# Writing the halves of the split weights for the gates, z and C 64 bytes further on than the others

## Chip, cores and metric

The kernel runs on one core of a Trainium2 chip. The metric is device time in microseconds (us) of one execution. The core has a matrix engine (TensorE; its matmuls are PE in the profile, its weight loads PEld), VectorE (DVE), ScalarE (ACT), GpSimd (POOL) and SyncE (SP, which issues most DMAs). A matmul here multiplies a *stationary* block of 128 x 128 values, which a weight load brings into the array first, by a *moving* block of 128 x N values that is streamed through it. The result is added into a bank of the accumulation memory.

## What is computed

Two layers over 256 latent tokens of width 2048 (and 256 context tokens, which only the first layer reads). In each layer the input is normalised, modulated and multiplied by a large weight matrix; the parts of the product go through different branches, and a second matrix brings the result back to 2048 columns.

```python
p = h @ w_in                      # layer 0: q, gate, z, k, v, x, B, C, dt: 14400 columns
pc = hc @ w_in[:, base:]          # the context needs k, v, x, B, dt
ya = neighbourhood_attention(q, k, v, kc, vc, rpb) * silu(gate)
yb = gated_group_rmsnorm(y_ssd + d * x, z, ssm_norm_g)
x = x + gate0 * (concat([ya, yb]) @ w_out)
...
bg, cg, hv, g = split(h1 @ sc_w_in, 4)        # layer 1
x = x + gate1 * ((silu(g) * bg * dw_conv(cg * hv)) @ sc_w_out)
```

The gates of the attention, z and C are needed for the 256 latent tokens alone; x, B, k and v for latent and context tokens, 512 in all.

## The kernel before

**Split operands.** Each fp32 operand of a large product is split in two fp32r halves: H, a rounded copy, and L, the rest. A product is the sum of three matmuls: H by H, H by L and L by H. Weights come from memory in blocks of 1024 values a partition (`raw`). ScalarE copies `raw` into an H half (L417), VectorE subtracts it from `raw` into an L half (L424).

**Places.** There are three places for split weights (`NW = 3`, L162). Place k has two tiles of 128 x 1024, `wH{k}` (L167) and `wL{k}` (L168), so all six tiles stand one behind the other in the on-chip memory, each 4096 bytes a partition. `place()` takes the next free one, `split()` (L398) writes H, `low_part()` (L421) writes L, and `used()` (L474) gives the place back when all matmuls of the block are issued. In the first output projection three more places are added (L1826): one is the two halves of a single tile, `KL`; another the tiles `QT` and `QL`; the third two reused tiles.

**Two ways to multiply.** `mm_act` (L640) keeps the activations in the array and streams the weights, 512 columns at a time. `mm_ws` (L650) does the opposite: a block of 128 weight columns is stationary and the activations `hH[kb]` or `hL[kb]` move, with n = 512 columns (latent and context) for x and B, and with n = 256 (latent) for the gates (`do_g`, L1486), C and z (both in `do_ssd`, L1491). So the gates, z and C are all the projections that `mm_ws` does with n = 256, and no other projection has that form. A group of attention heads has four gate blocks and four z blocks of 128 columns and two C blocks, times 16 blocks of the contraction, times 4 groups, times three products.

The only other split matmuls with 256 moving columns are those of the attention's last step (L1117 to L1119): there `VH` and `VL` are stationary and `PH`, `PL` move, 12 matmuls a head.

**Where tiles lie.** Tiles are laid out one behind the other in the order in which the code declares them. Nearly all sizes are multiples of 128 bytes, and so `wH`, `wL`, `hH`, `hL`, `PH`, `PL`, `KL`, `QT` and `QL` all start at a multiple of 128 bytes. `VH` and `VL` are declared after some small tiles (`statq`, `gqk` and others) and start 96 bytes behind such a multiple.

**Order of the work.** The program is one fixed list an engine, written out by a planner in Python. Projections form the main line; every matmul calls `pump()`, which puts in steps of other tasks (heads, groups of the scan, norms, the matrix-vector product of the modulation) when the planner's clock says that their inputs are ready. A task begins only when as many `tmp` and `half` tiles are free as it declares (`begin`, L213; `budget`, L202). There are nine `half` tiles (`NHALF`, L162). A `group_gen` (L1371; two for each group of heads) holds four, then three, then two; a head takes one for its product; `make_c` two; `dt_gen` three.

The output projection of layer 0 goes through its 16 pairs of blocks in the order written at L540: pairs 0 to 5, 8 to 15, then 6 and 7. Pair 15 is the product of the last `group_gen`. For the first 1024 output columns a pair takes 24 matmuls.

Of the kernel before, what the change touches and what calls it, by code (L numbers as in the profile page):

```python
# [9 lines left out]
F32R = mybir.dt.float32r  # L10
# [7 lines left out]
COL_Q, COL_G, COL_Z, COL_K, COL_V, COL_X = 0, 2048, 4096, 6144, 8192, 10240  # L18
COL_B, COL_C, COL_DT = 12288, 13312, 14336
# [122 lines left out]
def kernel(ctx: ExitStack, tc, x, cx, ada0, w0, ada_w, ada_b, w_in, w_out, sc_in, sc_out, rpb, small, const,  # L142
# [12 lines left out]
    def st(shape, tag, dt=F32, name=None):  # L155
        return sb.tile(list(shape), dt, tag=tag, name=name or tag, bufs=1)
# [2 lines left out]
        return dr.tile(list(shape), F32, name="dram_" + name)  # L159


    NTMP, NHALF, NRAW, NW = 9, 9, 5, 3  # L162
    free_t = [st([128, 512], f"tmp{k}") for k in range(NTMP)]
    free_h = [st([128, 256], f"half{k}") for k in range(NHALF)]
    free_b = [pj.tile([128, 512], F32, tag=f"bank{k}", name=f"bank{k}", bufs=1) for k in range(8)]
    free_r = [st([128, 1024], f"raw{k}") for k in range(NRAW)]
    WH = [st([128, 1024], f"wH{k}", F32R) for k in range(NW)]  # L167
    WL = [st([128, 1024], f"wL{k}", F32R) for k in range(NW)]  # L168


    xrow = [st([128, D], "KT", name="x0")]
# [33 lines left out]
    def spawn(q, gen, tmps=0, halves=0):  # L205
        q.append(Task(gen, tmps, halves))
# [155 lines left out]
    def issue():  # L362

        while (loads or later) and (free_r or (loads and callable(loads[0]))):
            if loads and callable(loads[0]):
                loads.popleft()()
                continue
            if later and (not loads or (ngem[0] < loads[0][7] and len(RAW) - ngem[0] >= 5 - loads[0][7])):
                kind, key, w, r0, nb, c0, n = later.popleft()
                ngem[0] += 1  # L370
            elif loads:
                kind, key, w, r0, nb, c0, n, _ = loads.popleft()
            else:
                return
            raw = raw_()
            v = raw[:, :nb * n].rearrange("p (b c) -> p b c", b=nb)
            if w is ada0 or w is w0:
                E(DMA.dma_start(raw, w[r0]))
            else:
                E(DMA.dma_start(v, w[r0:r0 + nb * 128, c0:c0 + n].rearrange("(b p) c -> p b c", p=128)))  # L380
            RAW[key] = (raw, v)

    nw = [0]
    room = [2]

    def weight(w, r0, nb, c0, n):
        loads.append(("w", nw[0], w, r0, nb, c0, n, room[0]))
        nw[0] += 1
# [5 lines left out]
    def place():  # L394
        in_use.append(free_w.popleft())
        return in_use[-1]

    def split():  # L398
        k = pos["split"]
        raw, v = RAW.pop(k)  # L400
        nb, n = v.shape[1], v.shape[2]
        w = place()
        if n == 64:

            while lows:
                low_part()
            W = WH[w].rearrange("p (b c) -> p b c", b=nb)
            E(S.copy(W[:, :, :64], v))
            E(V.tensor_tensor(out=W[:, :, 64:], in0=v, in1=W[:, :, :64].bitcast(F32), op=ALU.subtract))
            HL[k] = (W, None)  # L410
            pos["split"] += 1
            give_raw(raw)
            issue()
            return
        H = WH[w][:, :nb * n].rearrange("p (b c) -> p b c", b=nb)
        Lo = WL[w][:, :nb * n].rearrange("p (b c) -> p b c", b=nb)
        E(S.copy(H, v))  # L417
        lows.append((k, H, Lo, v, raw))
        pos["split"] += 1

    def low_part():  # L421

        k, H, Lo, v, raw = lows.popleft()
        E(V.tensor_tensor(out=Lo, in0=v, in1=H.bitcast(F32), op=ALU.subtract))  # L424
        HL[k] = (H, Lo)
        give_raw(raw)
        issue()
# [5 lines left out]
    def split_half(b):  # L433

        raw, v = RAW[0]
        H, Lo = (w[0].rearrange("p (b c) -> p b c", b=2) for w in (WH, WL))
        E(S.copy(H[:, b], v[:, b]))
# [13 lines left out]
    def splits_try():  # L451
        if hold[0]:
            return
        lows_try()
        while free_w and pos["split"] in RAW:
            if plan.ready([RAW[pos["split"]][1]]) > max(plan.t["PE"], plan.t["ACT"]) + 300:
                return
            split()
            lows_try()

    def use(ahead=0):
        k = pos["use"] + ahead
        while pos["split"] <= k:
            while pos["split"] not in RAW:
                issue()
                if pos["split"] not in RAW:
                    force(lambda: pos["split"] in RAW, (urgent, side, back))
            split()
        while k not in HL:
            low_part()  # L470
        splits_try()
        return HL.pop(k)
# [16 lines left out]
    def q_proj(w, c0, nc_, rows=D):  # L489
        room[0] = 2 if w is w_in and c0 >= COL_K else 1  # L490
        nb = 1024 // nc_
        for r0 in range(0, rows, nb * 128):
            weight(w, r0, nb, c0, nc_)

    def give_raw(raw):
        if not (spare_names and started[0] and raw.tensor.name in spare_names):
            free_r.append(raw)
# [34 lines left out]
    for j in range(1, 8):  # L532
        w_seg(j, CK, CV)
        if j < 7:
# [6 lines left out]
    ssd_cols = lambda s: [(w_in, COL_B + s * 256, 256), (w_in, COL_C + s * 256, 256), (w_in, COL_X + s * 512, 512),  # L541
                          (w_in, COL_Z + s * 512, 512)]
    q_proj(w_in, CG(0), 512)
    for r0 in (0, 1024):
        weight(w_in, r0, 8, COL_DT, 64)
    for j_ in ssd_cols(0)[1:]:
        q_proj(*j_)
    for a in range(1, 4):
        qk = [(w_in, CQ(a), 512), (w_in, CK(a), 512)]
        gv = [(w_in, CG(a), 512), (w_in, CV(a), 512)]  # L550
        for j_ in qk + gv + ssd_cols(a) if a < 3 else qk + ssd_cols(a) + gv:
            q_proj(*j_)
# [144 lines left out]
    def ada_gen():  # L697
        bc = lambda ap: ap.unsqueeze(2).to_broadcast([128, 2, 2])
        for j in range(8):
# [36 lines left out]
            for ts in ((0, 1), (2,), (3,)) if j == 0 else ((0, 1, 2, 3),):  # L736
# [25 lines left out]
                if ts == (0, 1):  # L762
                    hold[0] = False
                    split()
                    split()
# [854 lines left out]
    def turn_gen():  # L1620
        yield when(lambda: n_back[0] >= 11.5 and attn[0] == 32 and ssd_done[0] == 8)
        for k in range(2):
            pt = st([128, 4, 256], f"PT{k}", name=f"late{k}")
            late[4 * k:4 * k + 4] = [pt[:, q, :] for q in range(4)]
            pts.append(pt)
        E(V.scalar_tensor_tensor(out=A1, in0=M1[:, 1], scalar=1.0, in1=P_("g1"), op0=ALU.add, op1=ALU.mult))
        for kp in range(0, KB, 2):
            yield when(lambda: ("x1", kp // 4) in got and (kp < 8 or len(passed) == 4))
            yield W_("PE", x1[0][:, kp * 128:(kp + 2) * 128], x1[1][:, kp * 128:(kp + 2) * 128], nb=1)
            pt = bank()  # L1630
            for b in range(2):
                for t in range(2):
                    turn(pt[:, b * 256 + t * 128:b * 256 + (t + 1) * 128], x1[t][:, (kp + b) * 128:(kp + b + 1) * 128])
            if kp == 14:
                yield when(lambda: ("h1", 7, 0) in got)
            for b in range(2):
                kb = kp + b
                if kp < 8 or kp == 14:
                    yield W_("ACT", pt)
                    E(S.activation(late[kb], pt[:, b * 256:(b + 1) * 256], AF.Copy, scale=A1[:, kb:kb + 1]))  # L1640
                else:

                    held[kb] = pt
                got.add(("turn", kb))
            if kp < 8 or kp == 14:
                give(free_b, pt)
# [131 lines left out]
    for ns in ((0, 512), (1024,), (1536,)):  # L1778
# [41 lines left out]
        if len(ns) == 2:  # L1820
            force(lambda: attn[0] == 32 and not side)
            x1 += [st([128, D], "KT", name="x1a"), st([128, D], "Vt", name="x1b")]
            for H, Lo in ((KL[:, 0:2], KL[:, 2:4]), (QT, QL), (st([128, 4, 256], "gt", F32R, name="wH5"), st([128, 4, 256], "sz", F32R, name="wL5"))):

                free_w.append(len(WH))
                WH.append(H.rearrange("p a b -> p (a b)"))  # L1826
                WL.append(Lo.rearrange("p a b -> p (a b)"))
            spawn(side, turn_gen())
# [98 lines left out]
    for i in range(4):  # L1927
        for part, gen in ((1, cg_gen), (2, hv_gen), (3, gg_gen), (0, bg_gen)):
            ps = banks(2)
            kb0 = 0  # L1930
            if i == 0 and part == 1:
# [3 lines left out]
                for t in range(2):  # L1935
                    for kb in range(8):
# [3 lines left out]
                        H, Lo = ws[kb // 2]  # L1940
# [110 lines left out]
```

## Time and profile before

| | |
|---|---|
| runs (us) | 1775.3, 1775.44, 1772.64; median 1775.3 |
| profiled execution, first to last instruction (its span) | 1770.0 us |
| the same execution's time around the span | not on the page; the median lies 5.3 us above the span |
| PE busy | 1749.4 us, 99% |
| DVE busy | 1262.5 us, 71% |
| ACT busy | 773.7 us, 44% |
| granted TensorE clock, mean | 0.999 |

Busy time of PE is no measure of its pace: matmuls overlap in the pipeline, and one that shows 0.28 us can be followed by the next after 0.12 us. The pace of matmuls, from start to start, is read from the starts in the timeline, or from a piece of the chain of waits that holds nothing but matmuls: its length divided by their count.

### The profile page before, as it was taken

The page shows a single profiled execution, that of the slowest core. Times are in us where ns is not written, and L with a number is a line of the kernel's source. Part 1 is how long each engine was busy: PE and PEld are TensorE (multiplying, and loading weights), DVE is VectorE, ACT ScalarE, POOL GpSimd, SP SyncE. Part 2 cuts the span into 40 slices and gives each one's busy share as a digit, 9 for nine tenths or more (in the row PEclk, how much of TensorE's full clock was granted, in tenths as well). Part 3 has the DMA queues.
Part 4 walks back from the last instruction along what each step waited for, and adds up shares of the span by engine and source line. Part 5 has one row for each costly group of instructions (what it writes and reads, how often), then busy time and mean ns, then how long its engine had stood idle before and what let it go on. Part 6 is the DMA issues. An engine that isn't in the chain of part 4 may idle for free.

```text
span 1770.0 us, 25382 instructions
## 1 busy us (share of the span) xinstructions
PE 1749.4 (99%) x9577; PEld 1472.7 (83%) x9577; DVE 1262.5 (71%) x1986; ACT 773.7 (44%) x1330; POOL 31.3 (2%) x28
## 2 busy tenths in 40 slices
PE   6999999999999999999999999999999999999998
PEld 4777988888888889888888898888888888888887
DVE  5656788878686878775878777786668777555554
ACT  5423544455242445342445343564546344444442
POOL 0000100001000001000001000000000000000000
PEclk9999999999999999999999999999999999999999
DMA  9977644666746666655666556658867787666563
GB/s 362 348 284 255 208 148 142 194 203 202 232 140 200 200 195 200 207 148 185 205 191 191 160 174 213 189 184 286 284 224 242 250 259 253 207 188 190 190 211 119
DMA packets 218138, 374.60 MB, mean 212 GB/s; under 512 B 32304, under 2 KB 69008, under 8 KB 218016
## 3 DMA queue, kind: packets, MB, share of 16 engines
q1 hardware_dynamic: 210704, 366.38, 64.1%
q10 hardware_dynamic: 7312, 6.61, 1.2%
q8 instruction: 75, 1.23, 0.3%
q14 instruction: 47, 0.39, 0.1%
HBM read 367.52 MB, written 6.72 MB: 211 GB/s over the span
## 4 chain that ended last, share of the span: by engine, by line
PE 97%; DMA 1%; DVE 1%; ACT 0%; SPq 0%; issue 0%; POOL 0%; DVEq 0%; ACTq 0%
PE bank L192 94%; PE bank L196 3%; DMA tmp<-dram_csr 1%; DMA raw<-in_ada 0%; DVE wL L424 0%; DVE acc L812 0%; SPq L578 0%; DVE tmp L1405 0%; DVE tmp L1416 0%; DVE tmp L598 0%; ACT wH L417 0%; DVE acc L798 0%; DVE half L1443 0%; ACT tmp L1401 0%; ACT half L719 0%
## 5 line engine op out<-in xcount | busy, mean ns | idle before, releaser
L417 ACT CAST wH<-raw 128x1024 fp32r<-128x1024 f32 (+1 forms) x375 | 392.0, 1046 | 586.1 <-PE bank L192 493.1
L424 DVE TENSOR_TENSOR wL<-raw,wH 128x1024 fp32r<-128x1024 f32 (+1 forms) x374 | 453.4, 1215 | 219.5 <-ACT wH L417 217.9
L192 PE MATMUL bank<-hH,wH 128*128 128x256 f32 (+1 forms) x1040 | 342.9, 330 | 0.0
L192 PE MATMUL bank<-hL,wH 128*128 128x256 f32 (+1 forms) x1040 | 336.8, 324 | 0.0
L192 PE MATMUL bank<-hH,wL 128*128 128x256 f32 (+1 forms) x1024 | 331.1, 323 | 0.0
L192 PE MATMUL bank<-wH,hH 128*128 128x512 f32 x640 | 256.4, 401 | 2.6 <-ACT hH L752 2.6
L192 PE MATMUL bank<-wL,hH 128*128 128x512 f32 x640 | 250.1, 391 | 0.0
L192 PE MATMUL bank<-wH,hL 128*128 128x512 f32 x640 | 249.8, 391 | 0.1
L812 DVE SCALAR_TENSOR_TENSOR acc<-raw,csil,acc 128x512 f32<-128x512 f32 x256 | 191.7, 749 | 62.3 <-DMA raw<-in_ada_w 55.6
L192 PE MATMUL bank<-wH,h 128*128 128x512 f32 x680 | 215.7, 391 | 0.0
L192 PEld LDWEIGHTS bank<-hH,wH 128*128 128x128 f32 x1040 | 197.7, 190 | 17.0 <-issue 2.2
L192 PEld LDWEIGHTS bank<-hL,wH 128*128 128x128 f32 x1040 | 197.9, 190 | 15.0
L192 PEld LDWEIGHTS bank<-hH,wL 128*128 128x128 f32 x1024 | 194.6, 190 | 15.7 <-DVE wL L424 0.4
L192 PEld LDWEIGHTS bank<-wH,h 128*128 128x128 f32 x680 | 127.6, 188 | 26.6 <-issue 0.2
L192 PEld LDWEIGHTS bank<-wH,hH 128*128 128x128 f32 x640 | 120.6, 189 | 30.6 <-issue 4.6
L192 PEld LDWEIGHTS bank<-wH,hL 128*128 128x128 f32 x640 | 120.4, 188 | 25.5 <-DVE hL L758 0.6
L192 PEld LDWEIGHTS bank<-wL,hH 128*128 128x128 f32 x640 | 120.7, 189 | 23.9 <-DVE wL L440 0.3
L192 PE MATMUL bank<-wH,mix 128*128 128x512 f32 x432 | 137.9, 392 | 0.0
L192 PE MATMUL bank<-wL,h 128*128 128x512 f32 x340 | 132.3, 389 | 0.0
L192 PEld LDWEIGHTS bank<-wH,mix 128*128 128x128 f32 x432 | 81.1, 188 | 16.7 <-issue 0.2
L192 PE MATMUL bank<-wL,mix 128*128 128x512 f32 x216 | 84.1, 389 | 0.0
L192 PEld LDWEIGHTS bank<-wL,h 128*128 128x128 f32 x340 | 63.9, 188 | 12.9
(284 smaller groups left out, 2168.2 us busy)
## 6 DMA issues: line engine op xcount, KB each, us to landing
raw<-in_w_in SPq DMA_DIRECT2D x196, 512.0 KB, 3.9
raw<-in_ada_w SPq DMA_DIRECT2D x128, 512.0 KB, 4.7
raw<-in_sc_in SPq DMA_DIRECT2D x128, 512.0 KB, 3.7
raw<-in_w_out SPq DMA_DIRECT2D x64, 512.0 KB, 4.9
raw<-in_ada SPq DMA_DIRECT2D x36, 512.0 KB, 5.9
raw<-in_sc_out SPq DMA_DIRECT2D x32, 512.0 KB, 4.1
PT<-in_ada SPq DMA_DIRECT2D x16, 512.0 KB, 8.9
tmp<-dram_csr SPq DMA_DIRECT2D x32, 256.0 KB, 6.4
```

The costliest lines, as they stand in the source:

```text
L192: E(T.matmul(o, l, r, start=start, stop=stop, skip_group_check=True))
L196: E(T.transpose(o, i, ident if k == 128 else ident[:k, :k]))
L417: E(S.copy(H, v))
L424: E(V.tensor_tensor(out=Lo, in0=v, in1=H.bitcast(F32), op=ALU.subtract))
L812: E(V.scalar_tensor_tensor(out=acc, in0=v[:, j], scalar=csil[:, 2 * k + j:2 * k + j + 1], in1=acc, op0=ALU.mult, op1=ALU.add))
```

## The change

The two tiles of a place become one tile of 2112 values, whose first 1024 are the old `wH` and next 1024 the old `wL`; 64 values are spare. For weight blocks of the gates, z and C, whose numbers `q_proj` notes in `shifted`, both halves start 16 values (64 bytes) later in the place. To pay for the spare room there is one `half` tile less. The three places grow by 768 bytes together and the `half` tiles shrink by 1024, so every tile declared after the places stands 256 bytes earlier.

```diff
-    NTMP, NHALF, NRAW, NW = 9, 9, 5, 3
+    NTMP, NHALF, NRAW, NW = 9, 8, 5, 3
...
-    WH = [st([128, 1024], f"wH{k}", F32R) for k in range(NW)]
-    WL = [st([128, 1024], f"wL{k}", F32R) for k in range(NW)]
+    places = [st([128, 2112], f"w{k}", F32R) for k in range(NW)]
+    WH = [t[:, :1024] for t in places]
+    WL = [t[:, 1024:2048] for t in places]
+    shifted = set()
...
-        H = WH[w][:, :nb * n].rearrange("p (b c) -> p b c", b=nb)
-        Lo = WL[w][:, :nb * n].rearrange("p (b c) -> p b c", b=nb)
+        H, Lo = (places[w][:, 16:1040], places[w][:, 1040:2064]) if k in shifted else (WH[w], WL[w])
+        H, Lo = (t[:, :nb * n].rearrange("p (b c) -> p b c", b=nb) for t in (H, Lo))
...
         for r0 in range(0, rows, nb * 128):
+            if w is w_in and (COL_G <= c0 < COL_K or COL_C <= c0 < COL_DT):
+
+                shifted.add(nw[0])
             weight(w, r0, nb, c0, nc_)
```

The blocks for dt (64 columns) and the block that `split_half` writes (L433) use `WH` and `WL` and stay where they were in the place.

## The prediction

> **What bounds the kernel now.** I read the page first, for the engines' shares and the chain of work that ended last.
>
> ```profile
> span 1770.0 us, 25382 instructions
> PE 1749.4 (99%) x9577; PEld 1472.7 (83%) x9577; DVE 1262.5 (71%) x1986; ACT 773.7 (44%) x1330; POOL 31.3 (2%) x28
> PEclk9999999999999999999999999999999999999999
> PE 97%; DMA 1%; DVE 1%; ACT 0%; SPq 0%; issue 0%; POOL 0%; DVEq 0%; ACTq 0%
> ```
>
> The chain is PE for 97% of the span, at the full clock. So the time is the number of matmuls times their pace from start to start, and there is hardly a wait to take out. What the change can move is the pace, and only where it moves an operand. The groups of matmuls by form give the count of those it aims at, and of those in the attention's last step, which have the same form:
>
> ```profile
> L192 PE MATMUL bank<-hH,wH 128*128 128x256 f32 x640 | 184.1, 288 | 0.0
> L192 PE MATMUL bank<-hH,wL 128*128 128x256 f32 x640 | 181.1, 283 | 0.0
> L192 PE MATMUL bank<-hL,wH 128*128 128x256 f32 x640 | 181.0, 283 | 0.0
> L192 PE MATMUL bank<-PL,VH 128*128 128x256 f32 x64 | 17.9, 280 | 0.0
> ```
>
> In these names the moving tile stands first, the stationary one second. The gates, z and C are 3 x 640 = 1920 matmuls with 256 moving columns; their stationary operands are the shifted halves. Their pace comes from the pieces of the chain of waits that hold nothing else, the first in the z projection, the second at the end of the kernel, where 512 columns move:
>
> ```profile
> 300.18 20.16 PE bank L192 x168
> 1683.20 82.32 PE bank L192 x363
> ```
>
> 20.16 / 168 = 120.0 ns for 256 columns, 82.32 / 363 = 226.8 ns for 512. Half of the second is 113.4: a short one takes 6.6 ns more than half a long one. Is that a fixed cost, or something that depends on where the operands lie? The trace holds one group that answers: in the attention's last step the moving tiles start at a multiple of 128 bytes, as everywhere, but the stationary `VH` and `VL` start 96 bytes behind one. Two of its runs of 12 matmuls in the timeline, each with the long matmul ahead of it and the one after it:
>
> ```profile
> 493.71 0.40 PE L192 MATMUL bank<-hH,wL 128*128 128x512 f32 x1
> 493.94 0.28 PE L192 MATMUL bank<-PH,VH 128*128 128x256 f32 x1
> ...
> 495.23 0.28 PE L192 MATMUL bank<-PH,VL 128*128 128x256 f32 x1
> 495.34 0.40 PE L192 MATMUL bank<-KT,QT 128*128 128x512 f32 x1
> ```
>
> ```profile
> 1179.42 0.40 PE L192 MATMUL bank<-wH,mix 128*128 128x512 f32 x1
> 1179.66 0.28 PE L192 MATMUL bank<-PH,VH 128*128 128x256 f32 x1
> ...
> 1180.94 0.28 PE L192 MATMUL bank<-PH,VL 128*128 128x256 f32 x1
> 1181.05 0.40 PE L192 MATMUL bank<-wH,mix 128*128 128x512 f32 x1
> ```
>
> From the first of the 12 to the matmul after them: 1.40 and 1.39 us, so 116.3 ns each by the rounded starts (0.01 us on either end is 0.8 ns); I use 116.5. That is 3.5 ns under the 120.0 of the same form with an aligned stationary operand. The weight loads tell the two apart as well, first the z projection from 302 to 319 us, then the attention's step:
>
> ```profile
> L192 PEld LDWEIGHTS bank<-hL,wH x48: 192/192/192, 301.8 to 318.7; 128*128 128x128 f32 x48
> L192 PEld LDWEIGHTS bank<-PL,VH x64: 187/187/189, 269.5 to 1180.7; 128*128 128x128 f32 x64
> ```
>
> All loads of the aligned weights take 192 ns there, each the same, while those of the offset ones take 187 to 189. A load runs beside the matmul before it. My reading: with both operands in the same phase the load's reads and the matmul's reads get in each other's way in the same manner every time, and the pair locks at 120.0; with another phase it doesn't lock.
>
> **The change part by part.**
>
> *The shift itself* is 64 bytes, not 96. No row of before shows 64, so the pace is bounded from both sides. Lowest: 113.4 ns, half of the long matmuls. Highest: a long matmul that has a load of `VH` beside it is followed after 0.23 and 0.24 us in the two runs above, together 0.47 against 2 x 226.8 = 454 ns, some 8 ns each too much; charged to every one of the 1920, the pace would be 128. Unchanged at 120.0 is possible as well. I take 116.5, by the nearest row, the only one in which a short matmul has an offset load beside it: 1920 x 3.5 = 6.7 us off. From this I take a tenth, an estimate, since the locked pace isn't everywhere: the hH,wH group averages 288 ns against 283 for its two neighbours, 5 x 640 = 3.2 us of breaks where other work is put in, and these stay. That leaves 6.0 us.
>
> *Who has to keep up.* In two of the z stretches VectorE is nearly full:
>
> ```profile
> 302.00:320.00 18.00, 18.00 (x152) 18.00 (x152) 17.79 (x23) 9.93 (x13) 0.00 (x0) 1.00 0.50 149
> 1028.00:1048.00 20.00, 20.00 (x169) 20.00 (x168) 19.72 (x26) 10.27 (x12) 0.00 (x0) 1.00 0.54 160
> ```
>
> (Columns: PE, PEld, DVE, ACT, POOL busy.) VectorE has 0.21 of 18 and 0.28 of 20 us left, 1.3%, while PE would become 2.9% faster. If the subtractions have no lead there, some 1.6% of these 38 us, 0.6 us, can't be had, since the next L half would be late. The lead is not nothing, so I take half of it: 0.3 us.
>
> *One tile for both halves.* The kernel has such a place already, `KL`, and its copy and subtraction cost what those of two tiles do:
>
> ```profile
> L417 ACT CAST wH<-raw 128x1024 fp32r<-128x1024 f32 x370 | 388.9, 1052 | 577.8 <-PE bank L192 489.4 <-issue 53.6 <-DMA raw<-in_w_in 6.9
> L417 ACT CAST KL<-raw 128x1024 fp32r<-128x1024 f32 x32 | 33.7, 1054 | 45.6 <-PE bank L192 41.3 <-DMA raw<-in_sc_in 2.3 <-issue 1.8
> L424 DVE TENSOR_TENSOR wL<-raw,wH 128x1024 fp32r<-128x1024 f32 x369 | 450.0, 1222 | 219.5 <-ACT wH L417 217.9
> L424 DVE TENSOR_TENSOR KL<-raw,KL 128x1024 fp32r<-128x1024 f32 x32 | 39.2, 1224 | 21.2 <-ACT KL L417 21.2
> ```
>
> A shifted H half reaches over the first 64 bytes of the old L half. Its copy must therefore wait for the last matmul that read that L, one matmul (0.12 to 0.23 us) later than before, when the place changes from unshifted to shifted. ScalarE waits on PE at L417 in any case (489.4 us in the row) and has 56% of the span free; behind the copy in its queue stand evacuations that are a microsecond early or late without harm, and the block is needed only after those of the two other places, 2 x 24 x 0.12 = 5.8 us later, against 1.05 + 1.22 us for copy and subtraction. Cost: nothing; without that cover, 0.2 us at 36 changes at most (twelve stretches, three places), 7 us.
>
> *One half tile less.* Two `group_gen` at a time hold 4 + 4; a head's product is the ninth. By the bookkeeping in the code the last `group_gen`, which takes all four remaining halves, would find three and begin when the head at work gives one back. The heads' products of that stretch lie 6.5 us apart (1140.56 and 1147.03), so it begins some 6 us late at most. Its result is pair 15, 14th in the order, due after 13 x 24 = 312 matmuls of the output projection:
>
> ```profile
> 1140.56 0.42 ACT L945 CAST mix<-half 128x256 fp32r<-128x256 f32 x1
> 1147.03 0.41 ACT L945 CAST mix<-half 128x256 fp32r<-128x256 f32 x1 [3.34 <-DVE half L1123]
> 1202.52 0.76 DVE L947 TENSOR_TENSOR mix<-half,mix 128x256 fp32r<-128x256 f32 x2
> 1127.00:1203.30 76.30, 64.22 (x267) 49.28 (x268) 5.35 (x14) 5.08 (x14) 1.00 0.63 201
> ```
>
> When it is written, at 1203.3, 267 matmuls on `mix` have run; 45 more at 0.227 are 10 us of lead. A delay of 6 is hidden. With no lead it would cost those 6 us.
>
> *Everything behind the places moves by 256 bytes.* Phases within 256 bytes stay as they are for all unshifted weights. Two of the three places then stand half of 512 bytes from the activations, which no row shows; I take nothing, with 8 ns a load as the upper end, as for the shift. The planner's order may change in places, worth 1 us either way by the size of the few PE waits left (the chain has 1% of DMA and 1% of DVE).
>
> **The sum.** 1770.0 - 6.0 + 0.3 = 1764.3 us of span. The median of the runs is 5.3 above the span of the profiled execution; with that, 1769.6.
>
> **The rivals.**
>
> *The full pace.* The lock goes and nothing takes its place: 113.4 ns, 1920 x 6.6 = 12.7 us, less a tenth and up to 0.9 us for VectorE: 10.5, so 1764.8. For it: the long matmuls show that the array can stream so. Against: the offset loads of before don't reach it, on average.
>
> *Nothing.* 64 bytes may be the same phase as 0: then 120.0 stays and the time is 1775.3, give or take the planner's 1 us. For it: 96 is 32 behind 64, so the rows of `VH` would also fit a phase of 64 bytes. Against: 16 values is a strange amount to see nothing from, but no row excludes it. The Trainium skill ("TensorE: Matmul & The Clock Gate", "Step-by-step: what each phase is for") gives the same result on another ground: the engine has two independent read ports, and "Loading the next tile's weights doesn't steal SBUF read bandwidth from the running matmul." By that rule 64 bytes would change no pace; the 120.0 against 116.5 and the loads of 192 against 187 speak against it here, though runs of 12 are short.
>
> *Slower: the load taxes the matmul.* The 8 ns that a long matmul pays with a load of `VH` beside it are paid by each matmul with a shifted load beside it: 1920 x 8 = 15.4 us, 1790.7. It decides as soon as the pace passes 120.0; from 122 on (3.8 us in all) it can be measured. For it: both hand-overs, and weights of all long projections are left unshifted. Against: inside the two runs each of 11 matmuls has such a load beside it and takes 116.5.
>
> *Slower: a stall at pair 15.* The late `group_gen` loses its lead as well: 6 us, with no gain 1781; against it stands the lead of 10 us.
>
> **How the numbers follow.** The forecast 0.42; full pace 0.18; nothing 0.15; taxed loads 0.18; a stall or another loss in the order 0.07. A measurement of this kernel tells about 0.2% (3.5 us) from no change. Faster by more: the first two, 0.60. Within: 0.15. Slower: 0.25. The range reaches from 1762, below the full pace, to 1781, where the stall ends; the taxed loads (0.18) are left out. The likeliest case alone: 1766 to 1772.
>
> **What would show it.** Right: pieces of z and gates in the chain of waits at about 116.5 ns a matmul instead of 120.0, their weight loads under 192 ns, the long pieces still at 226.8, L417 and L424 at 1052 and 1222 ns, PE at 99%. Wrong: 120.0 and 192 as before (nothing), a pace over 122 (taxed), long pieces away from 226.8 (the 256 bytes), a PE gap before 1214 us (pair 15), or VectorE at 100% with PE waits on `wL` in the z stretches.

## The result, and the profile after

| | before | after |
|---|---|---|
| median of 8 runs on one chip | 1774.86 us (1772.64 to 1777.18) | 1769.30 us (1765.40 to 1772.62) |
| ratio after / before | | 0.9971, 95% interval 0.9961 to 0.9981 |
| span of the profiled execution | 1770.0 us | 1766.2 us |

The change makes the kernel faster by 0.29% (0.19 to 0.39%). The forecast was 1769.6 us and 1764.3 us of span. The sum therefore came out nearly right, but two of its terms did not, and they erred in opposite directions: the pace gave more than was reckoned, and more waits stand in the profile of after. Part of the latter is the chance of one execution, as the experiments show.

First the page of the changed kernel: span, engines, and the chain of work that ended last by engine.

```profile
span 1766.2 us, 25384 instructions
PE 1742.5 (99%) x9577; PEld 1464.8 (83%) x9577; DVE 1260.7 (71%) x1986; ACT 773.2 (44%) x1330; POOL 32.1 (2%) x28
PE 90%; DMA 5%; DVE 4%; issue 1%; SPq 1%; ACT 1%; POOL 0%; DVEq 0%; ACTq 0%
```

The same 9577 matmuls are busy for 6.9 us less. PE's share of the chain fell from 97% to 90%: the chain now leaves PE in places, through VectorE and a DMA. (This share alone is no sign of the change: the kernel without the shift, shown below, has 93%, and one that differs from the kernel before by 32 unused bytes has 90%.)

The pieces of the chain of waits (start, duration, what, how many) show the pace. The first is from a z projection, the second and the third are stretches of 90 and 102 short matmuls in gate projections, the last is the end of the kernel with 512 moving columns.

```profile
300.47 9.76 PE bank L194 x86
410.06 10.60 PE bank L194 x90
676.42 11.60 PE bank L194 x102
1679.35 82.32 PE bank L194 x363
```

9.76 / 86 = 113.5 ns, 10.60 / 90 = 117.8, 11.60 / 102 = 113.7, and 82.32 / 363 = 226.8 as before. So the short matmuls, nearly all of which ran at 120.0 before, now have **two paces**, 113.4 and 117.8, and the long ones are unchanged. The weight loads of the z projection, as the view of the tile shows them, have left the 192 ns as well:

```profile
L194 PEld LDWEIGHTS bank<-hH,w x45: 187/188/188, 301.9 to 309.4; 128*128 128x128 f32 x45
L194 PEld LDWEIGHTS bank<-hL,w x22: 187/188/188, 302.0 to 309.2; 128*128 128x128 f32 x22
```

Summed over the records of the trace from the start of each of the 1920 short matmuls to the start of the next, they took 233.6 us before and take 229.6 us now. These 4.0 us are the change of the span (3.8). But 3.0 us of standstill that the profile of before doesn't have are among the 229.6, so by pace alone some 7.0 us were won. The view of waits names the standstill (engine and line, what it waited for, us in total, times, longest); the first two rows are PE's, the last VectorE's from 180 to 245 us.

```profile
PE bank L194 <- ACT hH L757: 2.6, 2, 1.4
PE bank L194 <- DVE w L426: 2.5, 2, 1.8
...
DVE half L1161 <- DMA half<-in_rows: 6.1, 1, 6.1
```

The wait for L426, the subtraction that makes an L half, does not stand in the profile of before; the other PE row was there with the same 2.6 us. Its longer part in PE's timeline, with VectorE's timeline of the same stretch behind it:

```profile
235.60 0.28 PE L194 MATMUL bank<-hL,w 128*128 128x256 f32 x1
237.66 0.50 PE L194 MATMUL bank<-hH,w 128*128 128x256 f32 x2 [1.78 <-DVE w L426]
```

```profile
229.50 0.42 DVE L1159 TENSOR_TENSOR half<-bank,half 128x256 f32<-128x256 f32 x1 [0.46 <-ACT half L1157]
236.04 0.43 DVE L1161 TENSOR_TENSOR half<-half,half 128x256 f32<-128x256 f32 x1 [6.12 <-DMA half<-in_rows]
236.38 3.49 DVE L426 TENSOR_TENSOR w<-raw,w 128x1024 fp32r<-128x1024 f32 x3
```

VectorE stands for 6.12 us in front of one addition (L1161) that needs a small DMA of the dt rows, and three subtractions of L halves wait behind it in order. From start to start PE loses 1.9 us here. Before, the same place looked like this:

```profile
235.62 0.42 DVE L1156 TENSOR_TENSOR half<-half,half 128x256 f32<-128x256 f32 x1 [4.44 <-DMA half<-in_rows]
235.97 3.53 DVE L424 TENSOR_TENSOR wL<-raw,wH 128x1024 fp32r<-128x1024 f32 x3
```

VectorE stood there too, 4.44 us, and PE just did not notice: its matmul at 237.30 was the one that needed the L half finished some 0.1 us earlier (235.97 + 1.22 = 237.19, by the mean of L424). Now PE wants that half 1.6 us earlier, at 235.72, and it comes 0.4 us later. How much of this is the change's own is asked under "The new wait".

The second part is smaller and of another kind: at 841.54 the next matmul starts after 1.02 us, 0.9 late, since VectorE has six convolution steps (836.85, 4.53 us) ahead of the subtraction. The rest of the 3.0 is 0.17 us at 310 us, in a z projection.

### The profile page after: what moved, and what is told of

It reads as the page before. It is cut to its first block, busy times and chain, and to the rows that moved or that the text cites. A ratio compares the mean times of both kernels' runs of the same rounds, so it can differ in the third digit from the quotient of the medians.

```text
span 1766.2 us, 25384 instructions
## 1 busy us (share of the span) xinstructions
PE 1742.5 (99%) x9577; PEld 1464.8 (83%) x9577; DVE 1260.7 (71%) x1986; ACT 773.2 (44%) x1330; POOL 32.1 (2%) x28
## 4 chain that ended last, share of the span: by engine, by line
PE 90%; DMA 5%; DVE 4%; issue 1%; SPq 1%; ACT 1%; POOL 0%; DVEq 0%; ACTq 0%
PE bank L194 86%; PE bank L198 3%; DMA raw<-in_ada_w 2%; DVE acc L817 1%; DVE w L426 1%; DMA tmp<-dram_csr 1%; DMA raw<-in_w_in 1%; DMA raw<-in_ada 0%; DVE tmp L1241 0%; DMA raw<-in_sc_in 0%; DMA half<-in_rows 0%; SPq L1045 0%; DMA acc<-in_ada_b 0%; ACT w L419 0%; DVE tmp L981 0%
## 5 line engine op out<-in xcount | busy, mean ns | idle before, releaser
L419 ACT CAST w<-raw 128x1024 fp32r<-128x1024 f32 (+1 forms) x343 | 358.2, 1046 | 536.4 <-PE bank L194 458.9
L426 DVE TENSOR_TENSOR w<-raw,w 128x1024 fp32r<-128x1024 f32 (+1 forms) x343 | 414.8, 1213 | 179.7 <-ACT w L419 178.4
L194 PE MATMUL bank<-hH,w 128*128 128x256 f32 (+1 forms) x2064 | 489.2, 324 | 2.5 <-DVE w L426 2.5
L194 PE MATMUL bank<-w,hH 128*128 128x512 f32 x1280 | 405.8, 395 | 2.6 <-ACT hH L757 2.6
L194 PEld LDWEIGHTS bank<-hH,w 128*128 128x128 f32 x2064 | 345.0, 188 | 36.0 <-DVE w L426 3.5
L194 PE MATMUL bank<-hL,w 128*128 128x256 f32 (+1 forms) x1040 | 334.3, 322 | 0.0
L194 PEld LDWEIGHTS bank<-w,hH 128*128 128x128 f32 x1280 | 236.6, 188 | 54.6 <-issue 4.6
L194 PE MATMUL bank<-w,hL 128*128 128x512 f32 x640 | 249.3, 390 | 0.1
L194 PEld LDWEIGHTS bank<-hL,w 128*128 128x128 f32 x1040 | 196.4, 189 | 14.9
L194 PE MATMUL bank<-w,h 128*128 128x512 f32 x768 | 180.1, 391 | 0.0
L194 PEld LDWEIGHTS bank<-w,hL 128*128 128x128 f32 x640 | 120.1, 188 | 25.4 <-DVE hL L763 0.6
L426 DVE TENSOR_TENSOR wL<-raw,wH 128x1024 fp32r<-128x1024 f32 x31 | 37.9, 1222 | 27.6 <-ACT wH L419 27.5
L426 DVE TENSOR_TENSOR QL<-raw,QT 128x1024 fp32r<-128x1024 f32 x32 | 39.1, 1222 | 23.1 <-ACT QT L419 22.6
```

The source lines that it names most:

```text
L194: E(T.matmul(o, l, r, start=start, stop=stop, skip_group_check=True))
```

## The experiments

Each ratio is to the kernel before on the same chip, with its 95% interval. In all of them but the eight-halves and `VH` kernels the diff is against the changed kernel.

### Is it the shift?

The first kernel keeps everything of the change (the joint tile, one half tile less, all addresses) but never notes a block in `shifted`:

```diff
-            if w is w_in and (COL_G <= c0 < COL_K or COL_C <= c0 < COL_DT):
-
-                shifted.add(nw[0])
```

> The changed kernel with its layout, its eight half tiles and its order of instructions, but no block is shifted. Theory (phase): the gain comes from the 64 bytes alone, so the pieces of gates and z in the chain go back to 120.0 ns a matmul, all their weight loads to 192 ns, and the time to that of the kernel before, 1773 to 1777 us. Rival (layout and order): the gain comes from the places being 256 bytes elsewhere, one tile a place, or the changed order of work; then the time stays near 1769 us.

Measured: 1776.46 us, ratio 1.0009 (1.0000 to 1.0017). The order of the instructions is the changed kernel's; only addresses differ. Its z projections in the chain of waits and in the view of the tile:

```profile
300.19 20.16 PE bank L194 x168
410.72 10.79 PE bank L194 x90
```

```profile
L194 PEld LDWEIGHTS bank<-hH,w x96: 192/192/192, 301.9 to 319.0; 128*128 128x128 f32 x96
L194 PEld LDWEIGHTS bank<-hL,w x48: 192/192/192, 301.8 to 318.8; 128*128 128x128 f32 x48
```

The 120.0 ns and the 192 ns are back, to the digit. The gain is the shift's alone, and the places that moved by 256 bytes have the old pace: 256 bytes off is the same as 0.

The other part by itself, in the kernel before:

```diff
-    NTMP, NHALF, NRAW, NW = 9, 9, 5, 3
+    NTMP, NHALF, NRAW, NW = 9, 8, 5, 3
```

> The kernel before with eight half tiles instead of nine and nothing else; it puts the instructions in the order of the changed kernel. Theory: this order is what the kernel without a shift lost against the one before, so 1775.5 to 1777 us, with the same lateness of the last group's pair. Rival: the loss came from the one tile a place or from the addresses; then 1774.5 to 1775.3 us.

Measured: 1775.24 us, ratio 1.0000 (0.9989 to 1.0011). Its order is that of the changed kernel, so the whole difference in order between before and after comes from the half tile, and it costs nothing that can be measured. The loss that was expected of it (1775.5 to 1777 us) is not there.

### Which distances?

Only the shift differs, for instance for 32 bytes:

```diff
-        H, Lo = (places[w][:, 16:1040], places[w][:, 1040:2064]) if k in shifted else (WH[w], WL[w])
+        H, Lo = (places[w][:, 8:1032], places[w][:, 1032:2056]) if k in shifted else (WH[w], WL[w])
```

> The same blocks shifted by 32 bytes instead of 64. Theory (phase): any distance that isn't 0 ends the lock at 120.0; pace between 113.4 and 118 ns, time 1766 to 1772 us. Rival (whole lines of 64 bytes count): 32 bytes lie in the same line as 0, so 120.0 ns and 1775 us; or, with the halves now reaching over one line more, slower than 120.

> The same blocks shifted by 96 bytes, the distance that VH has in the kernel before. Theory (phase): the pace of the attention's last step, 116.5 ns with intervals from 113 to 120, and 1768 to 1771 us. Rival (runs of 12 are too short): the pace settles at 120.0 in long runs and the time is 1775 us.

> The same blocks shifted by 128 bytes. Theory (phase with a period of at most 128 bytes, since all aligned tiles of the kernel before lie at multiples of 128 and lock): 120.0 ns and loads of 192 ns come back, time as without a shift, 1775 to 1778 us. Rival (any distance but a multiple of 256 or 512 ends the lock): pace between 113 and 119, time 1768 to 1773 us.

> The same blocks shifted by 192 bytes. The runs so far: 120.0 ns at 0 (and at 256, for the places that stand that far off), 118.3 at 32, 113.4 or 117.8 at 64, 117.3 to 118.7 at 96, 118.4 to 120.4 at 128. Theory (a phase with a period of 256 bytes, and only the distance counts): 192 is 64 on the other side, so 113.4 or 117.8 again and 1768 to 1771 us. Rival (the direction counts): another pace, between 115 and 120, and 1771 to 1776 us.

> The same blocks shifted by 224 bytes, which is 32 on the other side: the distance, within 256 bytes, that VH has from PH in both kernels. Theory (only the distance counts): 118.3 ns as at 32, 1772 to 1774 us. Rival (the direction counts, and the rows of VH tell of this distance alone): 116.8 ns as in the attention's last step, 1769 to 1772 us.

The same two pieces of the chain of waits serve as the yardstick, the z projection of 168 matmuls and the stretch of 90. In order: 32, 96, 128, 192 and 224 bytes.

```profile
301.47 19.88 PE bank L194 x168
...
413.45 10.64 PE bank L194 x90
```

```profile
301.60 19.95 PE bank L194 x168
...
411.51 10.68 PE bank L194 x90
```

```profile
301.95 19.94 PE bank L194 x168
...
414.00 10.69 PE bank L194 x90
```

```profile
299.24 19.79 PE bank L194 x168
...
409.67 10.21 PE bank L194 x90
```

```profile
304.09 19.62 PE bank L194 x168
...
414.51 10.51 PE bank L194 x90
```

The two pieces are a sample. The column of the means takes in all stretches of short matmuls without a break, some 1830 intervals a run by the records of the trace.

| shift, bytes | ns a matmul, x168 | ns a matmul, x90 | mean of all stretches | ratio to before |
|---|---|---|---|---|
| 0 | 120.0 | 119.9 | 119.8 | 1.0009 (1.0000 to 1.0017) |
| 32 | 118.3 | 118.2 | 118.3 | 0.9989 (0.9980 to 0.9998) |
| 64 (the change) | 113.5 (x86) | 117.8 | 115.8 | 0.9971 (0.9961 to 0.9981) |
| 96 | 118.8 | 118.7 | 118.1 | 0.9996 (0.9985 to 1.0007) |
| 128 | 118.7 | 118.8 | 119.2 | 1.0001 (0.9991 to 1.0010) |
| 192 | 117.8 | 113.4 | 117.5 | 0.9974 (0.9964 to 0.9984) |
| 224 | 116.8 | 116.8 | 116.8 | 0.9978 (0.9965 to 0.9991) |

In these two pieces any distance but 0 and 256 ends the 120.0. Over all stretches 128 does so only in part: some 740 of its intervals stand in stretches that still average 120, a stretch of 192 matmuls among them. Only 64 and 192 reach 113.4, at 64 in nearly half of the intervals, at 192 in two stretches of 51 (the one of the table is the longer). By one theory 128 bytes would be a full period again. On the pace that fails for the stretches at 118.7 and stays open for the others, and so small a gain drowns in the time. The direction counts: 32 forward and 32 back (224) differ. The distance can't be told here from the stationary tile's own address, since the moving tiles of all the short matmuls start in the same phase of 256 bytes. Against the kernel before, the medians fall short of 1920 times the gain by one to three us, but for 192. Against the kernel with shift 0, which has the same layout and order, they agree with it within 2 us, and the intervals are no narrower than that.

The expectations held in part. The pace at 32 bytes lay just above its range, as did the time (1772.69 us). At 96 bytes both the pace and the time (1774.38) missed. At 128 some stretches have the pace of the theory and some that of the rival, and the time (1774.45) fits neither. At 192 the pace is that of the theory, with a time (1771.70) in the rival's range. At 224 the rival came true (116.8 ns, 1771.99).

### Does a load tax the matmul beside it?

Every block is shifted, also those of the projections with 512 moving columns:

```diff
-        H, Lo = (places[w][:, 16:1040], places[w][:, 1040:2064]) if k in shifted else (WH[w], WL[w])
+        H, Lo = (places[w][:, 16:1040], places[w][:, 1040:2064]) if w < NW else (WH[w], WL[w])
```

> All blocks in the three places are shifted by 64 bytes, but those of dt and the first. Theory (phase): a long matmul takes 226.8 ns, twice as long as a load, so a load's phase doesn't matter to it; pace of the long ones 226.8, time as with the change, 1768 to 1771 us. Rival (tax): long matmuls with a shifted load beside them take 8 ns more; x and B have 1184 of them, 9 us, time 1778 us or more.

Measured: 1785.61 us, ratio 1.0063 (1.0048 to 1.0078). The short matmuls keep the paces of the change (the 168 of the z projection 19.79 us, 117.8 ns). The long ones lose. Groups of matmuls by form, changed kernel first, then this one:

```profile
L194 PE MATMUL bank<-hH,w 128*128 128x512 f32 x784 | 256.5, 394 | 0.0
...
L194 PE MATMUL bank<-w,h 128*128 128x512 f32 x768 | 180.1, 391 | 0.0
...
L194 PE MATMUL bank<-hL,w 128*128 128x512 f32 x400 | 155.9, 390 | 0.0
```

```profile
L194 PE MATMUL bank<-hH,w 128*128 128x512 f32 x784 | 260.4, 398 | 0.0
...
L194 PE MATMUL bank<-w,h 128*128 128x512 f32 x768 | 182.0, 393 | 0.0
...
L194 PE MATMUL bank<-hL,w 128*128 128x512 f32 x400 | 157.9, 395 | 0.0
```

PE's order is the changed kernel's. From start to start, over the records of the trace, the 1184 with a shifted stationary operand (first and last row; 32 of them, in the first block, are not shifted) take 279.4 us in sum instead of 273.0, 5.4 ns more each, and those where the shifted weights move (as in the middle row) 2.5 ns more on average; the piece at the end of the kernel has such a rise in the chain of waits:

```profile
1695.83 83.03 PE bank L194 x363
```

83.03 / 363 = 228.7 ns against 226.8. 1184 x 5.4 = 6.4 us, and 3456 of the other kind (weights `w` with `hH`, `hL`, `h`, `mix` and `y`) x 2.5 = 8.6; together 15, and the kernel stands 16 us behind the change (10.6 us over its own before, against 5.6 under). So the tax that was seen at the two hand-overs is real, but it belongs to the long matmuls. For them the lock, or whatever it is, costs nothing, and breaking it costs 2.5 to 5.4 ns. The expectation's ground, that a long matmul is twice as long as a load, does not hold either: the loads last 187 to 192 ns in the views above, and 226.8 is not twice that.

Not all of the rise needs an operand that was moved. The 384 matmuls with `KL` as moving tile keep their addresses, and yet take 3.8 ns more on average: right behind a shifted block of weights the first ten of twelve start 224 to 236 ns apart, and only then is it 227 again. So a pace depends also on what ran just before.

The counter-test is in the kernel before: 32 unused bytes ahead of `VH` and `VL`, so that these stand at distance 0 as all other weights do.

```diff
+    st([128, 8], "fill")
     PHL, VHL = [], [st([128, 4, 128], f"V{k}", F32R) for k in "HL"]
```

> The kernel before with 32 unused bytes ahead of VH and VL, so that these start at a multiple of 128 bytes like PH and PL. Theory (phase): the 12 matmuls of the attention's last step take 120 ns instead of 116.5, 1.44 us a head, and the long matmul ahead of them hands over after 0.227 us instead of 0.235. Rival (another cause in that step): 1.40 us and 0.235 as before. The time within 1 us of before in either case.

One run, 1774.75 us, within 1 us of its before. The timeline of one group of twelve:

```profile
1182.11 0.39 PE L192 MATMUL bank<-wH,mix 128*128 128x512 f32 x1
1182.33 0.28 PE L192 MATMUL bank<-PH,VH 128*128 128x256 f32 x1
...
1183.64 0.28 PE L192 MATMUL bank<-PH,VL 128*128 128x256 f32 x1
1183.77 0.40 PE L192 MATMUL bank<-wH,mix 128*128 128x512 f32 x1
```

From 1182.33 to 1183.77 is 1.44 us, 120.0 ns each where it had been 116.3, and the long matmul hands over after 0.22 us where it had been 0.24. Over all 16 heads the mean rises from 116.7 to 119.5 ns by the records, and the usual hand-over falls from 235 to 227. Gain and tax both go when the address goes: this is the row of the prediction, switched off by 32 bytes.

### The new wait

If the dt rows arrive late since their DMA sits in SP's queue behind eight bias loads, another queue should take the wait away. The DMA is issued from ScalarE instead:

```diff
-        E(DMA.dma_start(rw[:, :128], rows[0].partition_broadcast(128)))
+        E(DMA2.dma_start(rw[:, :128], rows[0].partition_broadcast(128)))
```

> The changed kernel with the small load of the dt rows issued by ScalarE's queue instead of SyncE's, where it stands behind the loads of the heads' biases. Theory: the wait of 2.05 us at 235.6 us of the changed kernel, PE for VectorE's L half, which stands behind the wait for these rows, goes; 1 to 2 us faster than the changed kernel, 1767 to 1768.5 us. Rival: VectorE is the bound there and the wait moves on; 1769 us.

Measured: 1768.75 us, just above the time expected, ratio 0.9965 (0.9950 to 0.9980), span 1765.7. VectorE's timeline:

```profile
230.77 0.42 DVE L1159 TENSOR_TENSOR half<-bank,half 128x256 f32<-128x256 f32 x1 [1.14 <-ACT half L1157]
231.22 0.43 DVE L1161 TENSOR_TENSOR half<-half,half 128x256 f32<-128x256 f32 x1
231.72 1.23 DVE L426 TENSOR_TENSOR w<-raw,w 128x1024 fp32r<-128x1024 f32 x1
```

The load is now issued at 226.81 us instead of 230.44. The 6.12 us in front of L1161 are gone and so is PE's wait behind it; those at 310 us (0.17) and 841 us (0.76) are still there. Of the 2 us freed, the span keeps only 0.5, and the interval overlaps that of the change. So the cause of the wait is shown; that taking it away makes the kernel faster is not.

Whether the change made this wait is another question. The kernel with the aligned `VH` has the order of the kernel before on PE, and its projections run at 120.0 ns. Its execution shows the same wait; the first line is from VectorE's timeline, the second from PE's waits:

```profile
236.61 0.42 DVE L1157 TENSOR_TENSOR half<-half,half 128x256 f32<-128x256 f32 x1 [5.96 <-DMA half<-in_rows]
...
PE bank L192 <- DVE wL L424: 1.3, 1, 1.3
```

In the four profiled executions at 120.0 ns (the kernel before, eight halves, no shift, aligned `VH`) VectorE stands there for 4.44, 4.36, 4.95 and 5.96 us, and PE waits 0, 0, 0.28 and 1.30 us. So what goes beyond some 4.66 us reaches PE. With the change it is 6.12 and 1.78, and 4.34 us are covered. The faster pace is seen to take 0.3 us off the cover; the rest of this wait comes with rows that landed late in that execution, and in the profile of before they happened to land early. Whether the change also made them later is not shown. At the other place, 841 us, the same four have 0, 0.48, 0.20 and 0.15 us of wait, against 0.74 with the change. By these differences, and with the 0.17 us at 310, some 1 us of the 3.0 is the price of the faster pace, an estimate from single executions.

The planner reckons a short matmul at 9 + 0.434 x 256 = 120.1 ns. With the pace it now has, it might put the subtractions earlier:

```diff
-                return 9 + 0.434 * n, 190
+                return (116.0 if n == 256 else 9 + 0.434 * n), 190
```

> As the run before, and the planner reckons 116 ns instead of 120.1 for an fp32r matmul with 256 columns. Theory: side work of VectorE is put in less densely in the z stretches, so the waits of PE for L halves (1.0 us at 841.5, 0.3 at 310) go too: 1765.5 to 1767.5 us. Rival: the new order of the whole program costs more than it brings: 1768 to 1772 us.

Measured, with the DMA on ScalarE's queue as well: 1767.83 us, ratio 0.9958 (0.9945 to 0.9970), span 1767.0. That is between the time expected and the rival's. The waits at 310 and 841 us are gone, but a new one stands at 670 us, the longest of the first row. PE's waits by cause:

```profile
PE bank L194 <- DVE half L1455: 3.5, 2, 2.0
...
PE bank L194 <- DVE w L426: 0.7, 2, 0.6
```

What is left in the second row stands elsewhere, at 1125 and 1128 us.

It has the lowest median of all the kernels here, but its interval, too, overlaps that of the change; that it is better is likely and not shown.

## Why the prediction was right, and where it was not

**What bounds the kernel.** Right: the time moved with the pace of 1920 matmuls and with hardly anything else.

**The shift.** The mechanism was right in its main step: with the address of the stationary operand the pace changes, and without the shift nothing is left of the gain. How operand and load get in each other's way, as the prediction reads it, is not shown. The size, 116.5 ns, was right as a mean only. The stretches without waits average 115.8 ns (by the records, some 840 matmuls at 113 to 114 and 960 at 117 to 118). Neither pace is the 116.3 that I read from `VH`, and that row was no neighbour: its distance from its moving tile is 224 bytes, counted within 256, not 96. A shift of 224 gives 116.8 ns, as `VH` has; a shift of 96 gives 118.7 (118.1 over all stretches). That 64 bytes landed beside the value of 224 was luck. The lower bound, 113.4, is reached in 840 matmuls, so the rival of the full pace was nearly half there; the rival of no change was not, in any stretch.

**The tenth taken off** was about right: the stretches won 119.8 - 115.8 = 4.0 ns a matmul, 7.6 us for 1920, and pace alone brought 7.0. The term came out at 7.0 instead of 6.0 since the pace fell by 4.0 ns and not by 3.5.

**VectorE, 0.3 us.** This term was too small: 3.0 us in the profiled execution, of which some 1 us can be put down to the change. I looked for the place where VectorE is *busy* without a break, the z stretches. The view of windows there, changed kernel, columns as in the prediction:

```profile
302.00:320.00 18.00, 18.00 (x157) 17.73 (x156) 17.75 (x24) 10.24 (x13) 0.00 (x0) 1.00 0.51 148
1028.00:1048.00 20.00, 20.00 (x177) 19.98 (x176) 19.86 (x27) 10.79 (x15) 0.00 (x0) 1.00 0.60 172
```

PE starts 157 matmuls in place of 152 and 177 in place of 169, VectorE has 24 and 27 pieces of work in place of 23 and 26, and the loss in the first is 0.17 us. The large loss came where VectorE was *idle*, in order, in front of a late DMA, with 0.1 us of cover behind it. Its row (4.44 us for L1156) stood in the trace of before; I priced the engine's load and not its queue. But most of that loss would be there at the old pace too whenever the rows land as late, as they nearly did with the aligned `VH`. 1764.3 less 1.0 for the pace, plus 2.7 for the waits, is 1766.0, and the span is 1766.2.

**The span and the runs.** I added 5.3 us between one execution's span and the median; here the profiled execution took 1768.15 us in all, 1.95 over its span, and is 1.15 under its median. In every run on record the time is 1.8 to 2.2 us over the span. So most of the 5.3 was chance: the profiled execution of before, with 1770.0, was some 3 us faster than its median. That is why the spans differ by 3.8 us and the medians by 5.6, and why the time came out within 0.3 us, in part by luck, while the span was 1.9 off.

**Joint tile, half tile, 256 bytes.** Right, all at nothing: together they are the kernel without the shift, 1.0009 (1.0000 to 1.0017), at most 3 us, and the half tile alone is 1.0000. Copies and subtractions cost what they did:

```profile
L426 DVE TENSOR_TENSOR w<-raw,w 128x1024 fp32r<-128x1024 f32 x338 | 411.4, 1221 | 179.7 <-ACT w L419 178.4
```

There was no gap at pair 15.

**The taxed loads.** Refuted for this change and shown for a neighbouring one: with all blocks shifted the kernel is slower (1785.61 us), by 2.5 to 5.4 ns a matmul and for the long ones only. By the Trainium skill ("TensorE: Matmul & The Clock Gate", "Step-by-step: what each phase is for") the engine has two independent read ports, and a load takes no read bandwidth from the running matmul. That alone does not account for what is seen here: with the same instructions in the same order on PE, 64 bytes move a short matmul from 120.0 to 113.4 or 117.8 ns and lengthen a long one by 5.4.

**What stays open.** What the load and the moving operand share is not seen in any trace; "lock" is a name for a constant pace. What chooses between 113.4 and 117.8 is not settled, nor between the two paces at 96 bytes (117.4 and 118.7) and at 128 (118.6 and 120.0). It is fixed when a stretch begins and hardly changes within it. By the records of the changed kernel, all 13 stretches right behind a long matmul (226 ns to its successor) or behind a restart at 226 to 227 run at 117.4 to 117.9, and all 11 of more than ten matmuls whose first interval is 205 to 207 ns at 113.4 to 113.8; those that begin with 200 to 203 do either. No kernel was made that begins every stretch in one way.

## What to carry to other kernels

Where matmuls and weight loads alternate at the engine's limit, compare the pace of each shape with its share of the longest one (here 113.4 against 120.0), and if it is off, try moving the stationary tile by 64 bytes for that shape alone: here the shape at full pace lost by it. Measure the very distance and don't infer it from a neighbour: 32 bytes less or more lost most of the gain. When an engine at the limit gets faster, list the waits in order of the engines that feed it, long idle ones too, by how much cover is left at each; here the longest to show was not behind a busy VectorE but where the cover was thinnest. And compare such a wait over several executions before the change is charged with it.

## What the hardware showed that was not expected

- With the same instructions in the same order on PE, addresses alone make the medians 1769.3 (64 bytes for some blocks), 1776.5 (none) and 1785.6 us (all); by the ratios to before on each chip 0.9971, 1.0009 and 1.0063.
- The pace of a matmul with 256 moving columns is bistable at 64 bytes: 113.4 or 117.8 ns for whole stretches of up to 138 matmuls, with hardly anything between. At 192 bytes the same two paces occur, the faster in two stretches only.
- A shift of 64 bytes costs long matmuls and gains short ones: 5.4 ns more for 512 columns, 120.0 to 113.4 or 117.8 for 256.
- Long matmuls whose own operands did not move (`KL`) start 224 to 236 ns apart for some ten matmuls behind a shifted block, before 227 returns.
